# Two-layer hybrid decoder trunk: causal masks of four blocks moved to TensorE, linear unit's copies reordered, some low parts moved between VectorE and GpSimd

## Chip, cores and metric

One core of a Trainium2 chip. The time of an execution is device microseconds of the slowest core, here the only one. A kernel's time is the median of its runs. Some single executions were also recorded by the hardware profiler, and every row below comes from such a record.

## What is computed

Two residual layers over 1024 tokens of width 1024, all in float32 on the outside. In each layer the input is RMS-normalised, projected, mixed, gated, projected back and added.

```python
# layer 0: sliding-window attention and a state-space layer, side by side
ssm = s5_mixer(...) * silu(gate_b)       # s5_mixer ends with a gated linear unit:
#   h = gelu(y) @ glu_w + glu_b ;  h[..., :W] * sigmoid(h[..., W:])
h = h + concat([att * silu(gate_a), ssm]) @ w_out
# layer 1: an indexer scores all causal keys, the best 256 of each query are attended
score = sum_h w_h * relu(qi_h . ki)              # 8 index heads
_, idx = top_k(where(key <= query, score, -1e30), 256)
logits = where(valid, q . k * Dh**-0.5 + bias[query - key], -1e30)
h = h + (softmax(logits) @ v * silu(gate)) @ w_out
```

Layer 1 has 8 query heads of width 128 on 2 key heads. The kernel doesn't gather the selected keys. It computes the logits of all causal keys and adds a mask that makes those of unselected or later keys hugely negative.

## The kernel before

**Arithmetic.** Every float32 operand of a large matmul is split in two: `hi` is the operand rounded to the matmul's type (fp32r) and `lo = x - hi`. A product is three matmuls into one PSUM tile: hi.hi, hi.lo, lo.hi. So each operand costs a copy to `hi`, on ScalarE, and a subtraction for `lo`, on VectorE or GpSimd.

**Weights.** All weights come through one stream of 39 chunks of 1024 x 256 (class `Stream`, `load_w` at L134). The load goes to `wraw`; then `piece` writes `whi` on ScalarE (L153) and `wlo` (L154) on the engine that the tuple `LO_ON_V` (L126) names by the chunk's number: VectorE if the number stands there, GpSimd else. A chunk takes four pieces of 2 of its 8 rows of tiles (512 columns each). Chunks 0 to 8 are the input projection of layer 0, 9 and 10 the linear unit, 11 to 18 the output projection of layer 0, 19 to 30 the input projection of layer 1 and 31 to 38 its output projection. Within layer 1 the order is: two chunks for the indexer, then `PROJ1 = "a01kv23bcd"`, of which a to d are gate chunks and 0 to 3 query chunks. So chunk 22 is query chunk "0" and 23 is "1"; 24 and 25 are keys and values, 29 and 30 the gate chunks "c" and "d". The `hi` and `lo` of a chunk are made while the chunk before it is multiplied.

**Order.** TensorE's order is the program's own in the later stages (`manual_schedule`). The order of the other engines' instructions is laid out by a list scheduler which simulates a time line; `high_priority`, `behind(insts)` (L128, an instruction isn't queued ahead of those named) and `issue_after` bend it. Each engine then runs its queue strictly in order. All DMAs are issued by SyncE.

**The linear unit (L856 to L889).** Two chunks, each times two halves of the tokens, each times two tiles: eight groups of 24 matmuls of 512 columns (L872 to L874), two PSUM tiles a step. For each step ScalarE takes a tanh of one tile (L879), VectorE multiplies (L880, L881, the latter reading the second tile), ScalarE writes the high part (L882) and VectorE the low part (L883) of `cat[half]`, rows 4 to 7. In the list here a "GLU group" is one pass of `i` and `half`, two steps; they are counted 0 to 3, and groups 1 and 3 are the second half of the tokens. After the loop the attention branch's rows 0 to 3 of `cat` are loaded from DRAM (tile `at`, 4 buffers), copied on ScalarE (L888) and subtracted on VectorE (L889), eight times. Their pool is then closed, and the projection that follows (L895 to L925) loads the residual's tiles `xh` from DRAM into the space; VectorE adds a PSUM tile to one at L911. Its matmuls are L218 to L220 and L232 to L234, the helpers of all projections, in groups of 24.

**The indexer and the search.** TensorE makes the index scores (L1064, L1065), ScalarE the relu (L1067), VectorE the weighted sum (L1072), for blocks of 128 queries 2 to 7 (blocks 0 and 1 have at most 256 causal keys, so all are selected). Then a binary search of 32 steps finds each query's 256th score: blocks 3, 5, 7 on VectorE (class `OnV`, L1204; its count at L1221 writes a tile `vjunk` that nobody reads), blocks 2, 4, 6 on ScalarE and GpSimd (`OnS`, L1244; L1257, L1261). Bits of the scores are flipped ahead of it through a tile `flip` (L1198 to L1200). `tie_mask` (L1282) then writes `mk[b]`, bfloat16, 0 for a selected key and about 1e25 for another. All this runs beside the input projection of layer 1, whose head norms are made by ScalarE and GpSimd (`norm_heads`, L384: ScalarE squares at L389, GpSimd L199 and L200, ScalarE L392), and whose results are transposed on TensorE (L1151) and copied on ScalarE (L1153).

**Attention of layer 1.** A unit is a block of 128 queries with one of the two key heads, four query heads. `dsa_scores` (L1350): the bias of a head is loaded by a strided DMA into `bt`; GpSimd puts the mask into it, for blocks 0 and 1 by adding `mk0` to the diagonal's 128 columns (L1372), for others by subtracting `mk[b]` (L1374); TensorE makes the logits (three matmuls, L1375 to L1377, in one of 3 PSUM tiles `pq`); VectorE adds the bias, negates and takes the running minimum in one instruction (L1379); ScalarE takes the exponential (L1385); VectorE takes the reciprocal and, for two of four heads, normalises (L1390; ScalarE does the other two). Then TensorE transposes the probabilities (L1401), ScalarE and VectorE split them (L1404, L1405), and TensorE multiplies with the values (L1415 to L1417). The order of units: blocks 0 to 3 with key head 0, blocks 0 to 3 with key head 1, then blocks 4 to 7 with both. The scores of the first two units are made ahead (`first_units`, L1491, tiles of a pool `gat`), beside the projection of gate chunk "d". The scores of a later unit are made two units ahead of its values. `q1T_hi` and `q1T_lo` are the queries' parts (L1336 on ScalarE, L1337 on GpSimd for all but the first two units).

**Outputs.** The gated results of the first eight units are kept in tiles (`gat1`). At unit 8 `first_half` (L1595) closes the pool of the first half and calls `to_aT` (L1522) for all eight: ScalarE writes `aT_hi` (L1524), VectorE `aT_lo` (L1525), 512 columns each. The output projection of the first half (`out_pieces`, L1550 to L1552, 256 columns a matmul) then fills TensorE between the matmuls of blocks 4 to 7. Those of the second half call `to_aT` from `finish`.

## Time and profile before

| what | value |
| --- | --- |
| runs | 1068.32, 1062.63, 1068.51 us; median 1068.32 us |
| profiled execution | 1065.89 us, of which the recorded span is 1064.2 us |
| granted TensorE clock, mean of the span | 0.987 of full speed |
| busy share of TensorE / weight loads / VectorE / ScalarE / GpSimd | 95% / 84% / 70% / 58% / 41% |
| instructions | 19143 |
| DMA | 138.33 MB, mean 130 GB/s |

All times are microseconds from the start of the span unless marked ns. PE is the TensorE matmul, PEld its weight load (which overlaps), DVE VectorE, ACT ScalarE, POOL GpSimd, SP SyncE. A line L154 is line 154 of the kernel. In an instruction's row, `out<-in` are the program's tile names with partitions x elements; in square brackets stands the time for which the engine had been idle before it and the instruction that ended the idle time. `xN` counts instructions. Matmuls are pipelined, so that one's duration can be longer than the distance to the next, and some rows join several neighbours.

### The profile page before, as it was taken

How to read it: one execution, taken by the hardware profiler on the slowest of the kernel's cores; microseconds unless marked ns; L12 is line 12 of the kernel's file. 1: busy time of each engine (PE TensorE's matmuls, PEld its weight loads, DVE VectorE, ACT ScalarE, POOL GpSimd, SP SyncE). 2: the span in 40 equal slices, each digit the busy share in tenths (PEclk: the TensorE clock that was granted, in tenths of full speed). 3: DMA queues.
4: the chain of work that ended last, by engine and by line, in shares of the span. 5: the costliest groups of instructions: out<-in, count | busy, mean ns of one | idle time of the engine just before them, and what ended most of it. 6: DMA issues, size and time to landing. Idle time of an engine off the chain costs nothing.

```text
span 1064.2 us, 19143 instructions
## 1 busy us (share of the span) xinstructions
PE 1013.1 (95%) x6536; PEld 890.5 (84%) x6536; DVE 748.7 (70%) x1705; ACT 622.3 (58%) x1671; POOL 436.5 (41%) x722
## 2 busy tenths in 40 slices
PE   7899999999998999999999989999998889999998
PEld 5798999999864588877789989999886669898898
DVE  6628889973796554544667578888877986777742
ACT  7543653222787433434566989789967865565620
POOL 5897632221000002122041678678545847456000
PEclk9999999999999999999999999999999989999999
DMA  7282455339462317531020232122436644665333
GB/s 267 95 284 80 105 163 163 107 105 276 133 198 60 100 60 267 207 119 61 1 89 21 75 98 68 41 68 86 121 112 212 204 123 142 201 190 162 117 100 119
DMA packets 103697, 138.33 MB, mean 130 GB/s; under 512 B 9352, under 2 KB 79880, under 8 KB 98736
## 3 DMA queue, kind: packets, MB, share of 16 engines
q1 hardware_dynamic: 103600, 137.12, 41.3%
q8 instruction: 51, 0.84, 0.3%
q14 instruction: 46, 0.38, 0.1%
HBM read 102.31 MB, written 36.21 MB: 130 GB/s over the span
## 4 chain that ended last, share of the span: by engine, by line
PE 68%; DVE 14%; POOL 6%; ACT 5%; DMA 3%; issue 3%; SPq 1%; ACTq 0%; POOLq 0%; DVEq 0%
PE mm L234 8%; PE mm L232 8%; PE mm L233 8%; PE mm L218 5%; PE mm L219 5%; PE mm L220 5%; PE mm L1551 3%; PE mm L1552 3%; PE mm L1550 3%; PE psx L801 2%; PE tr L1401 2%; PE mm L1416 1%; PE mm L1417 1%; PE pq L1375 1%; PE tr L795 1%
## 5 line engine op out<-in xcount | busy, mean ns | idle before, releaser
L153 ACT CAST whi<-wraw 128x512 fp32r<-128x512 f32 (+1 forms) x152 | 87.3, 643 | 74.4 <-PE mm L233 38.2
L154 POOL TENSOR_TENSOR wlo<-wraw,whi 128x512 fp32r<-128x512 f32 x64 | 87.3, 1391 | 96.3 <-ACT whi L153 96.3
L219 PE MATMUL mm<-wlo,h1T_hi 128*128 128x256 f32 x384 | 110.3, 288 | 0.0
L218 PE MATMUL mm<-whi,h1T_hi 128*128 128x256 f32 x384 | 109.8, 288 | 0.2 <-DVE gst L981 0.2
L220 PE MATMUL mm<-whi,h1T_lo 128*128 128x256 f32 x384 | 109.6, 287 | 0.0
L1374 POOL TENSOR_TENSOR bt<-bt,mk 128x384 f32<-128x384 f32 (+3 forms) x80 | 82.5, 1049 | 61.9 <-DMA bt<-g_d 43.9
L919 POOL TENSOR_TENSOR acc<-acc,sq 128x512 f32<-128x512 f32 x12 | 18.1, 1507 | 195.4 <-DVE wlo L154 154.0
L1221 DVE TENSOR_SCALAR_CACHE_REDUCE vjunk<-sc,vt 128x512 bf16<-128x512 uint16 (+5 forms) x90 | 91.0, 1012 | 2.7
L232 PE MATMUL mm<-hT_hi,whi 128*128 128x256 f32 (+1 forms) x288 | 85.6, 297 | 0.0
L234 PE MATMUL mm<-hT_hi,wlo 128*128 128x256 f32 (+1 forms) x288 | 85.6, 297 | 0.0
L233 PE MATMUL mm<-hT_lo,whi 128*128 128x256 f32 (+1 forms) x288 | 85.5, 297 | 0.0
L1257 ACT ACTIVATE sjunk<-sc,st 128x384 bf16<-128x384 uint16 (+5 forms) x90 | 77.7, 864 | 6.2 <-POOL st L1261 4.2
L1550 PE MATMUL mm<-aT_hi,whi 128*128 128x256 f32 x256 | 73.5, 287 | 1.2 <-ACT aT_hi L1524 1.2
L218 PEld LDWEIGHTS mm<-whi,h1T_hi 128*128 128x128 f32 x384 | 72.9, 191 | 1.0 <-PE psi L1065 0.6
L219 PEld LDWEIGHTS mm<-wlo,h1T_hi 128*128 128x128 f32 x384 | 73.2, 191 | 0.4
L154 DVE TENSOR_TENSOR wlo<-wraw,whi 128x512 fp32r<-128x512 f32 (+1 forms) x88 | 62.9, 760 | 15.1 <-ACT whi L153 12.7
L1551 PE MATMUL mm<-aT_lo,whi 128*128 128x256 f32 x256 | 72.7, 284 | 0.7 <-DVE aT_lo L1525 0.7
L220 PEld LDWEIGHTS mm<-whi,h1T_lo 128*128 128x128 f32 x384 | 72.9, 190 | 0.4
L1552 PE MATMUL mm<-aT_hi,wlo 128*128 128x256 f32 x256 | 72.6, 284 | 0.0
L1385 ACT ACTIVATE s<-s,mn 128x384 f32<-128x384 f32 (+7 forms) x56 | 46.0, 821 | 30.9 <-DVE mn L1379 30.9
L1072 DVE SCALAR_TENSOR_TENSOR sc<-relu,wi,sc 128x384 f32<-128x384 f32 (+3 forms) x70 | 49.6, 711 | 20.3 <-ACT relu L1067 16.6
L392 ACT ACTIVATE st<-mm,nr 128x64 f32<-128x64 f32 (+1 forms) x160 | 46.0, 360 | 30.1 <-POOL nr L200 29.9
(398 smaller groups left out, 3478.7 us busy)
## 6 DMA issues: line engine op xcount, KB each, us to landing
wraw<-in_w_dram SPq DMA_DIRECT2D x20, 1024.0 KB, 5.0
wraw<-in_wo_dram SPq DMA_DIRECT2D x16, 1024.0 KB, 5.2
bt<-g_d SPq DMA_DIRECT2D x24, 256.0 KB, 4.6
g_d<-g1r_d SPq DMA_DIRECT2D x8, 576.0 KB, 10.8
bt<-g_d SPq DMA_DIRECT2D x24, 192.0 KB, 3.4
qT_d<-gst SPq DMA_DIRECT2D x32, 128.0 KB, 1.9
qT<-qT_d SPq DMA_DIRECT2D x32, 128.0 KB, 3.9
xh<-in_xT_dram SPq DMA_DIRECT2D x16, 256.0 KB, 5.7
```

What stands on the lines that cost most here:

```text
L153: S.copy(hi[p_], raw[p_])
L154: eng.tensor_sub(lo[p_], raw[p_], rd(hi[p_]))
L218: T.matmul(ps, a, hi[:, k, c0:c1], start=(k == 0), stop=False)
L219: T.matmul(ps, a, lo[:, k, c0:c1], start=False, stop=False)
L220: T.matmul(ps, b, hi[:, k, c0:c1], start=False, stop=(k == 7))
L232: T.matmul(o, a, hT[0][:, k, ts], start=(k == 0), stop=False)
L233: T.matmul(o, a, hT[1][:, k, ts], start=False, stop=False)
L234: T.matmul(o, b, hT[0][:, k, ts], start=False, stop=(k == 7))
L1221: V.tensor_scalar(junk[:, :128 * (b + 1)], data(b), self.thr(j), None, op0=OP.is_ge, op1=OP.add, accum_out=self.cnt[:, it, j:j + 1])
L1550: T.matmul(ps, a, aT[0][:, k, toks], start=(k == 0), stop=False)
L1551: T.matmul(ps, a, aT[1][:, k, toks], start=False, stop=False)
L1552: T.matmul(ps, b, aT[0][:, k, toks], start=False, stop=(k == 7))
```

## The change

Five edits:

1. `LO_ON_V` gets 22 and 23: the low parts of query chunks "0" and "1" are made on VectorE instead of GpSimd.
2. In the linear unit the instruction of the high and of the low part that each GLU group issued last is remembered. The copies and subtractions of the attention branch are queued behind those of group 1 (first half of the tokens) or group 3 (second half).
3. The unread output of the count on VectorE shares the tile `flip` instead of having `vjunk`.
4. The masks of blocks 0 and 1 become one bfloat16 tile of 128 x 256, 0 in its left half and 1e25 above the diagonal in its right one. For blocks 0 to 3 GpSimd no longer touches `bt`; the group of logit matmuls begins with one more, of the negated identity in bfloat16 with `mk[b]`, which puts the negated mask into PSUM. Blocks 4 to 7 stay as they were.
5. `to_aT` takes an engine for the low part; in `first_half` the first four of the eight units get GpSimd.

```diff
--- before.py
+++ after.py
@@ -123,7 +123,7 @@
 
     wcount = [0]
     raw_pools = [wp]
-    LO_ON_V = (0, 1, 2) + tuple(range(9, 21)) + (29, 30) + tuple(range(33, 39))
+    LO_ON_V = (0, 1, 2) + tuple(range(9, 21)) + (22, 23) + (29, 30) + tuple(range(33, 39))
 
     def behind(insts):
 
@@ -853,6 +853,7 @@
         ca = tuple(cps[1 - half].tile([128, 8, 512], F32R, name=f"cat_{n}") for n in ("hi", "lo"))
         cat.append(ca)
     gbt = yp.tile([128, 4, L], F32, name="gbt")
+    glu_last = []
     for n in range(4):
         dma(gbt[:, n], gb_d[n])
     for i in range(2):
@@ -879,14 +880,18 @@
                 S.activation(sg, pp[0], AF.Tanh, scale=0.5, bias=glub[:, 1, 4 + n:5 + n])
                 V.scalar_tensor_tensor(sg, sg, 1.0, gt_, op0=OP.add, op1=OP.mult)
                 V.scalar_tensor_tensor(sg, pp[1], glub[:, 0, n:n + 1], sg, op0=OP.add, op1=OP.mult)
-                S.activation(ca[0][:, 4 + n], sg, AF.Copy, scale=0.25)
-                V.scalar_tensor_tensor(ca[1][:, 4 + n], sg, 0.25, rd(ca[0][:, 4 + n]), op0=OP.mult, op1=OP.subtract)
+                glu_hi = S.activation(ca[0][:, 4 + n], sg, AF.Copy, scale=0.25)
+                glu_lo = V.scalar_tensor_tensor(ca[1][:, 4 + n], sg, 0.25, rd(ca[0][:, 4 + n]), op0=OP.mult,
+                                                op1=OP.subtract)
+            glu_last.append((glu_hi.ins, glu_lo.ins))
     for half in range(2):
         for g in range(4):
             at = st3.tile([128, 512], F32, name="at", bufs=4)
             dma(at, att_d[g, :, half * 512:(half + 1) * 512])
-            S.copy(cat[half][0][:, g], at)
-            V.tensor_sub(cat[half][1][:, g], at, rd(cat[half][0][:, g]))
+
+            with behind(glu_last[1 + 2 * half]):
+                S.copy(cat[half][0][:, g], at)
+                V.tensor_sub(cat[half][1][:, g], at, rd(cat[half][0][:, g]))
     es_y.close()
     es_3.close()
     es_h1 = ExitStack()
@@ -1217,7 +1222,7 @@
             if it % 16 == 0:
                 self.t = self.start()
             for j, b in enumerate(self.blocks):
-                junk = tk.tile([128, L], BF16, name="vjunk")
+                junk = tk.tile([128, L], I32, name="flip").bitcast(BF16)
                 V.tensor_scalar(junk[:, :128 * (b + 1)], data(b), self.thr(j), None, op0=OP.is_ge, op1=OP.add,
                                 accum_out=self.cnt[:, it, j:j + 1])
             i = it % 16
@@ -1317,11 +1322,15 @@
     if "sc7" in dbg:
         dma(dbg["sc7"], sc[7])
 
-    mk0 = mp.tile([128, 128], F32, name="mk0")
+
+    mk01 = mp.tile([128, 256], BF16, name="mk01")
     with tc.issue_after(ki_lo.ins):
-        G.memset(mk0, 0.0)
-    G.affine_select(out=mk0, in_=mk0, pattern=[[-1, 128]], compare_op=OP.is_ge, fill=NEG,
+        G.memset(mk01, 0.0)
+    G.affine_select(out=mk01[:, 128:], in_=mk01[:, 128:], pattern=[[-1, 128]], compare_op=OP.is_ge, fill=FAR,
                     base=0, channel_multiplier=1)
+    mk[0], mk[1] = mk01[:, 128:], mk01
+    nid = mp.tile([128, 128], BF16, name="nid")
+    V.tensor_scalar(nid, ident, -1.0, None, op0=OP.mult)
 
     def dsa_q_load(b, kv):
         qr = akv.tile([128, 4, 128], F32, name="q1r", bufs=2)
@@ -1367,12 +1376,12 @@
                     bp_ = fp if b < 4 and nbt[0] > 6 and nbt[0] % 2 else pool_
                     bt = bp_.tile([128, 512], F32, name="bt", bufs=6)[:, :n]
                 last_ttr[1] = dma(bt, skewed(h, 1023 - 128 * b + c0, n)).ins
-                with behind(last_rstd):
-                    if b < 2:
-                        G.tensor_add(bt[:, w - 128:], bt[:, w - 128:], mk0)
-                    else:
+                if b < 4:
+                    T.matmul(o, nid, mk[b][:, ks], start=True, stop=False)
+                else:
+                    with behind(last_rstd):
                         G.tensor_sub(bt, bt, mk[b][:, ks])
-                T.matmul(o, qT[0][:, g], kT[0][:, kv, ks], start=True, stop=False)
+                T.matmul(o, qT[0][:, g], kT[0][:, kv, ks], start=b > 3, stop=False)
                 T.matmul(o, qT[0][:, g], kT[1][:, kv, ks], start=False, stop=False)
                 T.matmul(o, qT[1][:, g], kT[0][:, kv, ks], start=False, stop=True)
 
@@ -1519,10 +1528,10 @@
     def gated(o, gv):
         V.scalar_tensor_tensor(gv, o, 0.5, gv, op0=OP.mult, op1=OP.mult)
 
-    def to_aT(b, kv, gv, aT):
+    def to_aT(b, kv, gv, aT, eng=V):
         qc = slice((b % 4) * 128, (b % 4 + 1) * 128)
         S.copy(aT[0][:, 4 * kv:4 * kv + 4, qc], gv)
-        V.tensor_sub(aT[1][:, 4 * kv:4 * kv + 4, qc], gv, rd(aT[0][:, 4 * kv:4 * kv + 4, qc]))
+        eng.tensor_sub(aT[1][:, 4 * kv:4 * kv + 4, qc], gv, rd(aT[0][:, 4 * kv:4 * kv + 4, qc]))
 
     def out_pieces(half, aT, ahead=None):
 
@@ -1597,8 +1606,8 @@
         ap_.append(es_a.enter_context(tc.tile_pool(name="att_l", bufs=1, reuse_waits="tile")))
         aT = attn_T()
         with tc.issue_after(last_ttr[0]):
-            for u in first:
-                to_aT(*u, aT)
+            for i, u in enumerate(first):
+                to_aT(*u, aT, G if i < 4 else V)
         fill.gen, fill.owed = out_pieces(0, aT), 0.0
 
     wstream.lazy = True
```

## Rows read from the trace of the kernel before

**Rows 1.** The page's first part: busy us, share of the span, instructions.

```profile
PE 1013.1 (95%) x6536; PEld 890.5 (84%) x6536; DVE 748.7 (70%) x1705; ACT 622.3 (58%) x1671; POOL 436.5 (41%) x722
```

**Rows 2.** The page's fourth part: the chain that ended last, by engine.

```profile
PE 68%; DVE 14%; POOL 6%; ACT 5%; DMA 3%; issue 3%; SPq 1%; ACTq 0%; POOLq 0%; DVEq 0%
```

**Rows 3.** By stage: length, busy per engine, granted clock, DMA share, GB/s.

```profile
621.00:630.00 9.00, 6.07 (x38) 5.74 (x37) 8.54 (x22) 5.05 (x18) 7.17 (x19) 0.81 0.46 147
626.00:790.00 164.00, 164.00 (x1167) 154.25 (x1166) 136.73 (x300) 144.19 (x428) 115.00 (x269) 0.99 0.25 79
811.20:866.50 55.30, 46.62 (x237) 36.74 (x238) 46.47 (x135) 41.45 (x102) 43.11 (x47) 0.94 0.66 208
866.50:878.00 11.50, 8.22 (x40) 7.32 (x39) 9.55 (x24) 7.91 (x16) 3.34 (x4) 0.70 0.38 103
```

**Rows 4.** Timelines of 353 to 412: start, duration, instruction, [idle before].

```profile
358.08 0.62 ACT L888 CAST cat_hi<-at 128x512 fp32r<-128x512 f32 x1 [5.26 <-DMA at<-att_d]
...
364.14 0.50 PE L872 MATMUL mm<-y_hi,whi 128*128 128x512 f32 x1 [2.19 <-DVE sg L881]
...
367.54 0.50 PE L872 MATMUL mm<-y_hi,whi 128*128 128x512 f32 x1 [0.34 <-ACT sg L879]
...
402.75 0.69 DVE L911 TENSOR_TENSOR xh<-mm,xh 128x512 f32<-128x512 f32 x1 [6.05 <-DMA xh<-in_xT_dram]
```

**Rows 5.** Steps of the chain that ended last: start, duration, line.

```profile
315.50 1.86 PE psx L801 x4
...
392.90 0.24 PE mm L232
```

**Rows 6.** GpSimd's timeline of 495 to 660, and TensorE's wait of 540 to 740.

```profile
545.47 5.77 POOL L154 TENSOR_TENSOR wlo<-wraw,whi 128x512 fp32r<-128x512 f32 x4 [5.40 <-ACT whi L153]
...
582.48 5.43 POOL L154 TENSOR_TENSOR wlo<-wraw,whi 128x512 fp32r<-128x512 f32 x4 [14.04 <-ACT whi L153]
...
PE tr L1151 <- ACT st L392: 2.9, 1, 2.9
```

**Rows 7.** VectorE: the group of L154 (busy us, mean ns) and its timeline near 550.

```profile
L154 DVE TENSOR_TENSOR wlo<-wraw,whi 128x512 fp32r<-128x512 f32 x84 | 58.0, 738 | 12.8 <-ACT whi L153 12.7
...
548.70 2.89 DVE L1072 SCALAR_TENSOR_TENSOR sc<-relu,wi,sc 128x320 f32<-128x320 f32 x2
552.24 1.20 DVE L1072 SCALAR_TENSOR_TENSOR sc<-relu,wi,sc 128x320 f32<-128x320 f32 x2
```

**Rows 8.** Groups and a wait of 811 to 866; the last row's group 785 to 811.

```profile
L1374 POOL TENSOR_TENSOR bt<-bt,mk 128x320 f32<-128x320 f32 (+2 forms) x30 | 28.2, 964 | 9.7 <-DMA bt<-g_d 9.2 <-DVE s L1390 0.3
...
L1337 POOL TENSOR_TENSOR q1T_lo<-q1r,q1T_hi 128x512 fp32r<-128x512 f32 x9 | 11.9, 1324 | 11.8 <-ACT q1T_hi L1336 11.8
...
L1372 POOL TENSOR_TENSOR bt<-bt,mk 128x128 f32<-128x128 f32 x8 | 3.6, 480 | 0.0
...
L1390 DVE TENSOR_SCALAR s<-s,den 128x384 f32<-128x384 f32 x4 | 4.1, 1047 | 0.0
...
L1390 DVE TENSOR_SCALAR s<-s,den 128x256 f32<-128x256 f32 x2 | 1.7, 849 | 0.1
...
DVE s L1379 <- POOL bt L1374: 1.3, 2, 0.7
...
L1390 DVE TENSOR_SCALAR gat<-gat,den 128x256 f32<-128x256 f32 x2 | 0.6, 352 | 0.0
```

**Rows 9.** TensorE's timeline of 809 to 813.

```profile
811.24 0.44 PE L1375 MATMUL pq<-k1T_hi,q1T_hi 128*128 128x384 f32 x1 [1.33 <-ACT q1T_hi L1336]
```

**Rows 10.** Timelines of 850 to 878: TensorE, VectorE and GpSimd.

```profile
869.80 0.41 PE L1375 MATMUL pq<-k1T_hi,q1T_hi 128*128 128x320 f32 x1 [1.39 <-DVE mn L1379]
872.62 0.79 PE L1416 MATMUL mm<-pT_lo,v_hi 128*128 128x512 f32 x1 [1.89 <-DVE pT_lo L1405]
...
868.06 1.28 DVE L1525 TENSOR_TENSOR aT_lo<-gat,aT_hi 128x512 fp32r<-128x512 f32 x2
...
872.10 0.79 POOL L1374 TENSOR_TENSOR bt<-bt,mk 128x320 f32<-128x320 f32 x1 [5.71 <-DVE aT_lo L1525]
```

## Prediction

> **What bounds the kernel now.** I read the page's busy shares first: TensorE has work in 95% of the span [rows 1], so only time in which TensorE waits, or runs at its lower clock, can be won, and every matmul that is added has to find such time. The chain that ended last says where that time is: 68% of it is TensorE, 14% VectorE, 6% GpSimd [rows 2]. The table by stage then shows that the lost time is not spread evenly. From 626 to 790 us TensorE is busy in all 164.00 us: nothing done there on other engines can shorten it, and what is won ahead of it is carried through. Three of the places that the change touches lose: 621 to 630 (TensorE busy 6.07 of 9 us, mean granted clock 0.81), the attention of the first four blocks (811.2 to 866.5, 46.62 of 55.3, clock 0.94) and the stretch in which the first half's outputs are split (866.5 to 878, 8.22 of 11.5, clock 0.70) [rows 3]. The fourth, the linear unit, I read wait by wait in the timelines of its engines [rows 4]; the prices of single instructions come from the groups by line and the waits of a stage.
>
> **A, the linear unit's order.** ScalarE stands in program order in front of the first att copy (L888) for 5.26 us until its load has landed; behind it queue L882 and L879, on VectorE L883 and L881, and those free the PSUM tiles. So TensorE waits 2.19 us for L881 at 364.14 and 0.34 us for L879 at 367.54 [rows 4]. With the att copies queued behind GLU groups 1 and 3 both waits go: 2.5 us. What is late instead: the last four copies and four subtractions now follow the last GLU step, some 4 x 0.6 = 2.4 us, and the load of `xh` may wait that long for their tiles. Its first use on VectorE already waits 6.05 us, until 402.75 [rows 4], but TensorE needs a PSUM tile back only three groups of 24 matmuls after 392.90, the start of the projection on the chain: 3 x 24 x 0.24 (the 512-column matmul there [rows 5]) = 17.3 us, at 410.2. That leaves 7 us for the 2.4. **A = -2.5 us**; with the cover gone it would be 0.
>
> **B, chunks 22 and 23 on VectorE.** Counting the four-piece bursts of L154 on GpSimd from chunk 21 on, 22 is the burst at 545.47, 23 the one at 582.48 and 24 the next. They hold GpSimd for 5.77 and 5.43 us [rows 6], and the head norms (L199, L200) queue behind it. From 582 to 625 the chain runs beside TensorE: burst 23, then norms, then ScalarE, then burst 24, then norms, until TensorE gets a transpose after a wait of 2.9 us [rows 6]; the granted clock then falls, mean 0.81 over 9 us, which is 9 x 0.19 = 1.7 us of lost columns [rows 3]. Without burst 23 ScalarE and GpSimd are up to 5 us earlier at burst 24, more than the 2.9 us by which they were late. VectorE pays 8 pieces x 0.74 = 5.9 us [rows 7]. But its own instructions are slowed while GpSimd runs a burst: two of 320 columns take 2.89 us at 548.70 against 1.20 us at 552.24, behind the burst [rows 7], so about 1.7 us a burst, 3.4 us in two, comes back. The net 2.5 us falls before 613, where VectorE waits for ScalarE's relu anyway. Bounds: -4.6 (all of 2.9 + 1.7) to +1 (VectorE holds the relu tiles up near 545). I take -4.0, near the full sum, since the late norms have one visible cause. **B = -4.0 us.** Sharing the tile `flip` adds no wait of an engine on another: counts and flips are both VectorE's. At worst the first counts of two blocks move behind the last flip (under 2 us), which TensorE, fully busy there, doesn't see.
>
> **C, the masks on TensorE.** Removed: 32 additions on GpSimd. In the stage 811 to 866 that is 8 of L1372 and 16 of the 30 of L1374 [rows 8], together 8 x 0.48 + 16 x 0.96 = 19 us of an engine that was busy 43.11 of 55.3 [rows 3]. GpSimd itself is rarely waited for (DVE for bt 1.3 us, [rows 8]); the gain is on VectorE, busy 46.47 of 55.3. Its normalisation L1390 takes 849 ns for 256 columns in this stage against 352 ns for the same shape ahead of it, and 1047 ns for 384 [rows 8]. The two of 256 lose 0.5 us each; the four of 384, with 0.45 us (an estimate, a little above the 352) as their own price, 0.6 each; with what the smallest lose I put 4 us. With the 1.3 us wait that is 5.3 us of VectorE, and VectorE holds much of the chain here.
>
> The Trainium skill (SBUF — State Buffer, "SBUF: two separate sides") says that VectorE and GpSimd take a shared port pair by an exclusive lock, held for a whole instruction. The trace agrees for L1390 (849 against 352 ns). By that rule the subtractions that the change puts on GpSimd lock VectorE out in their turn, which is rival 2: the time would be its 1059.4 us instead of the 1054.7 that I take.
>
> Added: 32 matmuls, 4 x 2 x (128 + 256 + 384 + 512) = 10,240 columns, bf16 on bf16, a kind that no row shows. Cheap end: 0.24 us for 512 columns; dear end: 1.86 / 4 = 0.465 us, as the slowest 512-column matmul [rows 5]: 4.8 to 9.3 us. I take the cheap end, as the masks enter beside matmuls that keep that pitch at the full clock. Of it 1536 columns, 0.7 us, fall to the first two units (795 to 804), where TensorE then waits 1.33 us at 811.24 for ScalarE anyway [rows 9], so about 0.3 us counts; the other 4.1 us fall into the stage, where TensorE has 55.3 - 46.6 = 8.7 us idle. About a third of the chain there is TensorE's, so 1.4 to 2 us of it count. **C = -5.3 + 1.8 + 0.3 = -3.2 us**, bounds -9 to +6.
>
> **D, four low parts on GpSimd.** VectorE's eight L1525 stand between TensorE and what it waits for: 1.39 us for L1379 at 869.80 and 1.89 us for L1405 at 872.62; four of them (two took 1.28 us at 868.06 [rows 10]) are 2.5 us. After the waits the clock is low (mean 0.70 to 878), 11.5 x 0.3 = 3.5 us. Full gain: 2.5 + about 2 of clock. Against it: GpSimd takes 1.32 us for this subtraction [rows 8], 5.3 us for four. It is idle for 5.71 us up to 872.10 [rows 10], so its queue bears them, but VectorE's remaining four would run beside them, and L1390's 849 against 352 ns tells what that can cost. I take **D = -2.0 us**, bounds -5 to +2.
>
> **Sum.** -2.5 - 4.0 - 3.2 - 2.0 = -11.7 us against the profiled execution's 1065.9 us (span 1064.2 and 1.7 around it): 1054.2. The median of the three runs is 2.4 us above that execution and the lowest 3.3 below; I add half a microsecond and say 1054.7 us, of which the range holds the doubt.
>
> **Rivals.** 1. The masks set TensorE's pace (slower side). Each group's first matmul now stands on the path from a freed PSUM tile to VectorE. A matmul that starts behind a wait took 0.50 us [rows 4]; the stage gets 24, 12.0 us, VectorE then waits for TensorE, and its 5.3 us are worth nothing. With D void too and the first two units at 1.4 us: -2.5 - 4.0 + 12.0 + 1.4 = +6.9, 1073.3 us. It decides from the point where a mask matmul costs over 0.29 us on the path (7 us / 24). For it: TensorE is at 95%. Against: 8.7 us idle in the stage.
>
> 2. The port: GpSimd's 5.3 us in D lock out VectorE's four L1525 and the L1390 beside them, and q1T_lo and the other bt go on doing so in the stage: C gives 0 and D 0. Then A + B = -6.5, 1059.4 us. For it: 849 against 352 ns. Against: the masks, most of GpSimd's work there, go.
>
> 3. The relief is worth more: VectorE's chain in the stage shortens by its whole 5.3 us and TensorE's lower clock (0.94 x 55.3: 3.3 us) mostly goes, D gives 4.5: -2.5 - 4.6 - 8 - 4.5 = -19.6, 1046.3 us.
>
> 4. A does nothing, because the late `xh` loads make TensorE wait what it saved: -9.2, 1056.7 us.
>
> **How the numbers follow.** Forecast 0.50 (own range 1049 to 1060), rival 1 0.12, rival 2 0.18, rival 3 0.12, rival 4 0.08. The range 1045 to 1068 leaves out the upper part of rival 1 and a little below rival 3. One per cent is about what a measurement of this kernel can tell from no change; against the median of 1068.3 it lies at 1057.6. Faster by more: 0.38 of the forecast, all of rival 3, half of rival 4: 0.54. Slower by over 1% (1079) needs rival 1 and a bad new order besides: 0.06. The rest, 0.40, is within 1%.
>
> **What would show it.** A: no wait at L872, the last L889 near 395. B: the 2.9 us wait at L1151 gone, clock 1.0 from 600 to 790, bursts of L154 on VectorE. C: L1390 near 350 ns for 256 columns, the stage 811 to 866 some 3 us shorter, mask matmuls at 0.23 us for 512 columns. D: no wait of TensorE above 1 us where the outputs are split, and a clock above 0.85 there. The forecast is wrong if the stage of the first blocks gets longer, or if a new wait of TensorE stands between 626 and 790.

## The result, and the profile after

The changed kernel takes 1058.26 us (median of 7 runs, 1055.13 to 1060.39) against 1067.86 us for the kernel before in the same comparison (7 runs, 1062.63 to 1069.52): ratio 0.992, 95% interval 0.9899 to 0.9941. That is 9.6 us less by the medians, 8.5 by the ratio. The forecast was 1054.7 us in a range of 1045 to 1068; of the three chances it falls to "within 1%", by a little.

The page of the changed kernel, its first and fourth part:

```profile
PE 1009.5 (96%) x6568; PEld 888.7 (84%) x6568; DVE 748.0 (71%) x1710; ACT 621.6 (59%) x1671; POOL 403.7 (38%) x686
...
PE 70%; DVE 13%; POOL 5%; DMA 4%; ACT 4%; issue 3%; SPq 1%; ACTq 0%; POOLq 0%; DVEq 0%
```

TensorE has 32 matmuls more, GpSimd 36 instructions and 32.8 us less [rows 1]. The stages that answer to [rows 3], moved by TensorE's lead (columns as there):

```profile
616.00:625.00 9.00, 6.75 (x43) 6.42 (x42) 8.58 (x21) 6.48 (x24) 7.24 (x21) 0.81 0.45 147
621.00:785.00 164.00, 164.00 (x1165) 154.23 (x1165) 140.11 (x304) 142.83 (x425) 110.97 (x264) 0.99 0.24 78
806.70:859.30 52.60, 47.65 (x263) 37.32 (x264) 43.98 (x135) 41.84 (x103) 23.48 (x24) 0.97 0.68 215
859.30:870.80 11.50, 7.51 (x41) 6.64 (x40) 9.15 (x20) 7.62 (x15) 9.71 (x9) 0.85 0.36 101
```

The first row is a surprise: the stretch that part B was to mend still has a granted clock of 0.81. The third is shorter by 3.0 us (811.2 to 866.8 took 55.6 before). The last has a better clock, yet TensorE is busy for less of it.

Where the time went is best read from four instructions that every kernel here has, by their starts in the timelines. I take the first matmul of the projection behind the linear unit (L232, 392.7 before), the first logit matmul of all (L1375, 795.1), the ninth, with which the stage of the first blocks begins (811.2), and the one that is the 41st, the first of block 4 with its second key head (866.8). Each is given as its distance from the one ahead of it, the first from the linear unit's restart at 353.3, the last column up to the start of the last matmul:

| kernel | linear unit | to first logits | first units | first blocks | behind them |
| --- | --- | --- | --- | --- | --- |
| before | 39.4 | 402.4 | 16.1 | 55.6 | 193.9 |
| changed | 36.4 | 399.7 | 16.9 | 52.6 | 193.4 |
| linear unit alone | 36.5 | 403.4 | 16.0 | 54.9 | 192.7 |
| chunks alone | 39.2 | 401.3 | 20.2 | 55.0 | 192.5 |
| masks alone | 40.5 | 402.4 | 17.8 | 53.4 | 192.8 |
| split alone | 40.3 | 400.8 | 16.1 | 54.5 | 195.1 |
| changed, low parts all on VectorE | 36.5 | 399.7 | 16.9 | 53.3 | 192.8 |
| changed, low parts all on GpSimd | 36.5 | 399.6 | 16.9 | 53.1 | 196.8 |
| linear unit + chunks | 36.5 | 401.5 | 17.3 | 55.0 | 194.3 |
| changed + chunk 24 | 36.5 | 395.2 | 25.5 | 54.6 | 193.4 |
| the same, search one step shorter | 36.5 | 395.4 | 16.6 | 53.2 | 195.8 |

Each row is one profiled execution. Up to the linear unit the executions differ by -1.1 to +2.9 us though nothing there was changed, which is why the stages are compared and not the spans, and a stage still scatters by a microsecond or two, as its clock falls once more or less. So, from the unrounded starts, the changed kernel won 3.1 us in the linear unit, 2.7 up to the first logits and 3.0 in the first blocks, lost 0.7 in the first units, and won 0.5, which is nothing, behind them.

### The profile page after: what moved, and what is told of

It reads as the page before. It is cut to its first block, busy times and chain, and to the rows that moved or that the text cites. A ratio compares the mean times of both kernels' runs of the same rounds, so it can differ in the third digit from the quotient of the medians.

```text
span 1056.1 us, 19160 instructions
## 1 busy us (share of the span) xinstructions
PE 1009.5 (96%) x6568; PEld 888.7 (84%) x6568; DVE 748.0 (71%) x1710; ACT 621.6 (59%) x1671; POOL 403.7 (38%) x686
## 4 chain that ended last, share of the span: by engine, by line
PE 70%; DVE 13%; POOL 5%; DMA 4%; ACT 4%; issue 3%; SPq 1%; ACTq 0%; POOLq 0%; DVEq 0%
PE mm L234 8%; PE mm L232 7%; PE mm L233 7%; PE mm L218 4%; PE mm L219 4%; PE mm L220 4%; PE mm L1560 3%; PE mm L1561 3%; PE mm L1559 3%; PE tr L1410 2%; PE psx L801 2%; PE mm L1425 1%; PE mm L1426 1%; PE pq L1384 1%; PE pq L1386 1%
## 5 line engine op out<-in xcount | busy, mean ns | idle before, releaser
L154 POOL TENSOR_TENSOR wlo<-wraw,whi 128x512 fp32r<-128x512 f32 x56 | 76.5, 1394 | 76.7 <-ACT whi L153 76.7
L1226 DVE TENSOR_SCALAR_CACHE_REDUCE flip<-sc,vt 128x512 bf16<-128x512 uint16 (+5 forms) x90 | 91.0, 1012 | 2.6
L1383 POOL TENSOR_TENSOR bt<-bt,mk 128x320 f32<-128x320 f32 (+3 forms) x64 | 66.8, 1060 | 58.0 <-DMA bt<-g_d 36.3
L232 PE MATMUL mm<-hT_hi,whi 128*128 128x256 f32 (+1 forms) x288 | 85.6, 297 | 0.0
L154 DVE TENSOR_TENSOR wlo<-wraw,whi 128x512 fp32r<-128x512 f32 (+1 forms) x96 | 66.1, 732 | 14.3 <-ACT whi L153 13.9
L392 ACT ACTIVATE st<-mm,nr 128x64 f32<-128x64 f32 (+1 forms) x160 | 45.7, 357 | 27.8 <-POOL nr L200 27.6
L1413 ACT CAST pT_hi<-tr 128x512 fp32r<-128x512 f32 x72 | 41.5, 578 | 33.9 <-PE tr L1410 31.9
```

Of the source, the lines that this page charges most:

```text
L154: eng.tensor_sub(lo[p_], raw[p_], rd(hi[p_]))
L232: T.matmul(o, a, hT[0][:, k, ts], start=(k == 0), stop=False)
L1226: V.tensor_scalar(junk[:, :128 * (b + 1)], data(b), self.thr(j), None, op0=OP.is_ge, op1=OP.add, accum_out=self.cnt[:, it, j:j + 1])
```

## The experiments

**1. The linear unit's order alone.** L880 to L889 as in the change, nothing else.

```diff
-                S.activation(ca[0][:, 4 + n], sg, AF.Copy, scale=0.25)
+                glu_hi = S.activation(ca[0][:, 4 + n], sg, AF.Copy, scale=0.25)
...
+            with behind(glu_last[1 + 2 * half]):
```

> The kernel before with the linear unit's new order alone. My theory: the two waits at L872 (2.19 and 0.34 us) go and nothing takes their place, so the run is 2.5 us under the kernel before, and TensorE is ahead by 2.5 us when the output projection of layer 0 begins and keeps this to the end. Rival (the late loads of xh take it back): no wait at L872, but TensorE's lead is gone at 420 us and the time is that of the kernel before. Second rival (the gain is given back at the wait for L392 near 625, which GpSimd's bursts set): the lead of 2.5 us holds to 610 and falls under 1 us by 640.

Measured: 1062.32 us against 1066.33, ratio 0.9963 (0.9943 to 0.9982). The two waits at L872 [rows 4] are gone: TensorE's waits from 340 to 400 us are down to one line (what waited, for whom; total, times, longest):

```profile
PE tr L795 <- DVE pT L798: 1.5, 2, 0.9
```

The stage is 2.9 us shorter. Counted from the linear unit's restart, TensorE is still 2.0 us ahead at the ninth logit matmul (3.1 by the spans' own times, of which 1.1 were there before the stage began). My theory holds in the main and the first rival falls. The second names a place where about 1 us is given back: the wait for L392 is 2.9 us as before, but the mean granted clock behind it, from 620.1 to 626.9, is 0.50, where before it was 0.75 from 625.4 to 632.2. That is one execution, and the lead did not fall under 1 us.

**2. The chunks alone.**

```diff
-    LO_ON_V = (0, 1, 2) + tuple(range(9, 21)) + (29, 30) + tuple(range(33, 39))
+    LO_ON_V = (0, 1, 2) + tuple(range(9, 21)) + (22, 23) + (29, 30) + tuple(range(33, 39))
```

> The kernel before with the low parts of chunks 22 and 23 on VectorE and nothing else. In the changed kernel the wait at L1151 stayed (2.3 us) and so did the stretch at the lower clock behind it; ahead of it stands the burst of chunk 24 on GpSimd, and the search has been put beside it. My theory: the burst of chunk 24 owns that wait, so this edit brings 1 to 2.5 us, and the wait at L1151 is still over 2 us. Rival (as predicted): the wait was owned by the burst of chunk 23; without the other edits' shift the wait and the lower clock go, and the run is 4 us faster.

Measured: 1068.71 against 1066.33 us, ratio 1.0011 (0.9994 to 1.0029): no gain. TensorE's waits at L1151 were 4.5 us in all, so the rival falls. But 1.1 us were won up to the first logits, and 4.1 lost again in the first units. There TensorE waits 2.05 us for VectorE, and from 798.7 to 805.5 the mean granted clock is 0.50 (1.00 over the same 6.8 us before), which is 6.8 x 0.5 = 3.4 us of columns. That place was in neither theory.

**3. The masks alone** (with the shared `flip`).

```diff
+                if b < 4:
+                    T.matmul(o, nid, mk[b][:, ks], start=True, stop=False)
...
-                junk = tk.tile([128, L], BF16, name="vjunk")
+                junk = tk.tile([128, L], I32, name="flip").bitcast(BF16)
```

> The kernel before with the masks of blocks 0 to 3 on TensorE and the shared tile flip (the masks' tiles need its space). My theory: the first two units cost 1 us more, the stage of the first blocks gets 3 us shorter because VectorE's normalisation no longer runs beside GpSimd's mask work; together 2 to 3 us under the kernel before, and the normalisation of 256 columns near 0.58 us. Rival (the port's relief needs the other edits, the masks alone only load TensorE): the stage is not shorter and the run is 0 to 2 us above the kernel before.

Measured: 1066.18 against 1066.33 us, ratio 1.0 (0.9977 to 1.0023). Neither theory is clean: the first blocks got 2.2 us shorter, as in mine, but the first units took 1.7 us longer.

**4. The split alone.**

```diff
-                to_aT(*u, aT)
+                to_aT(*u, aT, G if i < 4 else V)
```

> The kernel before with four of the eight low parts of the first half's outputs on GpSimd and nothing else. My theory: VectorE's other four take 1.3 us each instead of 0.64 while GpSimd works, so VectorE is done no sooner and the wait for L1405 grows as much as the wait for L1379 shrinks: 0 us, within half a microsecond either way. Rival (the prediction's): VectorE's queue is 2 us shorter and TensorE's waits between 866 and 878 fall from 3.3 to about 1 us: 2 us faster.

Measured: 1066.32 against 1066.33 us, ratio 0.9996 (0.9977 to 1.0014). The two waits of [rows 10], 3.3 us, became one of 3.6 us for L1405, as in my theory.

**5 and 6. The changed kernel with all eight low parts on VectorE, and all eight on GpSimd** (`V`, or `G`, in place of `G if i < 4 else V`).

> The changed kernel with all eight low parts of the first half's outputs back on VectorE. My theory (the split gains nothing, because each of VectorE's low parts beside GpSimd's takes twice its time): the time of the changed kernel within 1 us, TensorE's waits between 857 and 870 again some 3.3 us in two pieces. Rival (the split is worth 2 us): 2 us above the changed kernel.

> The changed kernel with all eight low parts on GpSimd. My theory: GpSimd needs 8 x 1.47 = 11.8 us, VectorE's few instructions beside it each wait for one of GpSimd's, and the mask subtractions of block 4 and the first output matmul queue behind: TensorE waits 4 us or more longer than in the changed kernel, 3 to 7 us slower. Rival (VectorE's queue was the only thing in the way): VectorE is free 4.6 us sooner, the wait for L1414 (3.6 us in the changed kernel) goes, and the run is 2 to 3 us faster.

Measured against the same runs of the kernel before (1065.58 us): all on VectorE 1059.21, ratio 0.9946 (0.9924 to 0.9968); all on GpSimd 1060.31, ratio 0.9949 (0.9926 to 0.9971). Both lie 2.8 to 3.1 us above the changed kernel's 0.992 by the ratios, with overlapping intervals, so these times alone don't exclude that the split is worth 2 us. The traces speak against it: with all eight on VectorE the waits are back as 1.37 and 1.89 us, where the split has one of 3.62, and the stretch behind the first blocks is no longer (192.8 against 193.4 us).

With all eight on GpSimd the wait of 3.62 us is gone, as in the rival, but a longer one comes 15 us later. VectorE, GpSimd and TensorE:

```profile
871.57 8.18 DVE L1399 TENSOR_SCALAR s<-s,den 128x640 f32<-128x640 f32 x1
...
881.40 0.55 DVE L1399 TENSOR_SCALAR s<-s,den 128x640 f32<-128x640 f32 x1
...
877.61 1.79 POOL L1383 TENSOR_TENSOR bt<-bt,mk 128x384 f32<-128x384 f32 x2
...
880.87 0.79 PE L1425 MATMUL mm<-pT_lo,v_hi 128*128 128x512 f32 x1 [5.78 <-DVE pT_lo L1414]
```

One normalisation on VectorE takes 8.18 us, the next of the same shape 0.55. It ends at 879.75; GpSimd worked from 861.03 to 879.40 without a gap that the profile shows, its queue of low parts, masks and weights being longer now. In no other trace here does an instruction of this kind take over 1.8 us. The stretch behind the first blocks is about 3.5 us longer than in the changed kernel, as I expected (3 to 7), but this execution (1063.53 us) is 3.2 us above the median of its 12 runs, and against all eight on VectorE the ratios differ by 0.3 us only. How often the long wait comes, these runs don't show.

**7. Chunk 24 on VectorE too.**

```diff
-    LO_ON_V = (0, 1, 2) + tuple(range(9, 21)) + (22, 23) + (29, 30) + tuple(range(33, 39))
+    LO_ON_V = (0, 1, 2) + tuple(range(9, 21)) + (22, 23, 24) + (29, 30) + tuple(range(33, 39))
```

> The changed kernel with the low parts of chunk 24 on VectorE too. My theory: the burst of L154 at 611 on GpSimd owns the wait of 2.3 us at L1156; without it the head norms come in time, the wait and the lower clock behind it (1.7 us) go: 3 to 4 us under the changed kernel. Rival (VectorE becomes the one that is late, as it is busy 9.5 of 10 us there): the wait stays over 1.5 us, now behind VectorE's L154, or moves to the next chunk; within 1 us of the changed kernel.

Measured: 1065.57 against 1065.58 us, ratio 1.0008 (0.999 to 1.0027). The whole gain of the changed kernel is gone, although the wait at L1156 and the low clock behind it went, as my theory said: TensorE led by 9.4 us at the first logits and by 0.1 at the ninth.

**8. Without the mask matmuls** (the masks of blocks 0 to 3 are left out of the computation).

```diff
-                if b < 4:
-                    T.matmul(o, nid, mk[b][:, ks], start=True, stop=False)
...
```

> The changed kernel without the mask matmuls: the masks of blocks 0 to 3 are left out of the computation. It prices the 32 matmuls. My theory: their 10,240 columns at 0.23 us for 512 are 4.7 us of TensorE's time, of which about half lies in waits: 2 to 3 us under the changed kernel, near 1 us of it in the first two units. Rival (they set TensorE's pace): 5 us or more under it. Other rival (hidden in waits for VectorE): within 1 us.

Measured: 1057.76 us, ratio 0.9927 (0.9901 to 0.9953), the changed kernel's 0.992. The 32 matmuls are hidden: the first units take 16.3 us without them and 16.9 with them, the first blocks 52.8 and 52.6. The rival that they are hidden holds.

**9. Linear unit and chunks, without masks and split** (the edits of 1 and 2 together).

> The kernel before with the linear unit's new order and chunks 22 and 23 on VectorE, without the masks and the split. Alone, the order brought 4.0 us and the chunks lost 1.2 us. In the run of the chunks alone TensorE had won 1 us by 789 and lost 4.9 between 789 and 803, where VectorE, in the middle of the chain of the selection masks, stood 4.1 us for a TensorE group. First theory (that loss comes from where the scheduler puts the last gate's and the first units' instructions among the mask chain, and the masks on TensorE change this): the loss returns, and the run is about 3 us under the kernel before. Second theory (the loss came from TensorE being late against the mask chain by chance of that order, and the linear unit's order mends it): TensorE leads by 5 us at 789 and keeps it at 812; 5 to 7 us under the kernel before, and the masks and the split add 2 to 3 us more to make the changed kernel.

Measured: 1065.94 against 1067.44 us, ratio 0.9985 (0.9967 to 1.0003). The first theory is the nearer one: the 5 to 7 us of the second lie outside the interval. But of the loss in the first units 1.2 us returned, not 4.1; TensorE's wait for VectorE is there again (2.05 us), the low clock of experiment 2 is not (mean 1.00 from 794 to 812). By the two ratios the chunks take back more than half of what the linear unit brought, though the intervals of experiments 1 and 9 overlap. Masks and split together, worth nothing alone, make the step from 0.9985 to 0.992; the changed kernel without the split stands at 0.9946 (experiment 5), so by the ratios more than half of the step is the masks' edit.

**10. The selection masks in another order.**

```diff
-    for b in range(2, NT):
+    for b in ON_V + ON_S:
         tie_mask(b, *found[b])
```

> The changed kernel with the selection masks made in the order 3, 5, 7, 2, 4, 6 instead of 2 to 7. VectorE's searches end 5.7 us before ScalarE's (763.2 against 768.9), so the chain of masks can start sooner. My theory: that chain (L1297 to L1307) sets when the second unit's queries can be split (q1T_hi, 0.6 us behind the last mask in every run so far) and with it the stage of the first blocks. Its end comes 3 to 5 us sooner, but TensorE's own work ends 1.35 us before that, so only 1 to 2 us are won: 1 to 2 us under the changed kernel. Rival (TensorE's own work sets it): the wait for q1T_hi is gone or the same, and the time is within half a microsecond of the changed kernel. Second rival (ScalarE's search is delayed by the mask instructions put among it): the last mask is no sooner, 0 to 2 us slower.

Measured: 1063.1 us, ratio 0.9966 (0.9945 to 0.9986): slower than the changed kernel. The last mask came no sooner (805.3 against 805.7), although the search was not delayed (it ended at 769.0 instead of 768.9), and TensorE stood 3.84 us for VectorE in the first unit. The second rival named the effect, but neither its cause nor its size.

**11. Experiments 7 and 10 together.**

> The changed kernel with chunk 24 on VectorE too and the masks in the order 3, 5, 7, 2, 4, 6. With chunk 24 alone TensorE led the kernel before by 9.5 us at 789 and by nothing at 812: it waited 2.7 us for VectorE and 5.1 us for q1T_hi, behind the mask chain. My theory (the chain is the wall): with the chain earlier the lead is kept in part, and the run is 4 us or more under the run with chunk 24 alone, about the time of the changed kernel or 1 to 3 us under it. Rival (chunk 24 loads VectorE and ScalarE, and these are slower whatever the order): the lead is lost again between 789 and 812 and the run is within 1.5 us of the one with chunk 24 alone.

Measured: 1062.83 us, ratio 0.9956 (0.994 to 0.9972), against 1.0008 with chunk 24 alone. The lead at the ninth logit matmul was 2.8 us instead of 0.1, as the last mask came at 807.9 instead of 810.6. So the lead is kept in part, as in my theory, but the run stays above the changed kernel, where I had expected its time or less. TensorE still waits 5.82 us for `q1T_hi` there.

**12. Chunk 24, and the search one step shorter.**

```diff
-    for it in range(16, 32):
+    for it in range(16, 31):
...
```

> The changed kernel with chunk 24 on VectorE too and the binary search one step shorter (31 of 32 steps; the last bit of each query's threshold is left out of the computation). A step takes 251 us / 32 = 7.8 us on ScalarE's side. My theory (search and mask chain are the wall that takes chunk 24's gain): the last mask comes 6 to 8 us sooner, the wait for q1T_hi (5.1 us) goes, TensorE keeps 6 us or more of its lead of 9.5 us at 812; 5 us or more under the run with chunk 24 alone and 1 to 4 us under the changed kernel. Rival (TensorE loses it through VectorE's order around the first units): the waits for VectorE stay, and the run stays within 2 us of the one with chunk 24 alone.

Measured: 1057.02 us, ratio 0.9903 (0.9876 to 0.993). What changed is the wait for the end of the search: the last mask is done at 802.8 instead of 810.6, the wait for `q1T_hi` fell from 5.1 to 1.0 us, that of 2.7 us for VectorE in the first unit went too, and TensorE kept 7.5 of its 7.9 us of lead. This is my theory. Against the changed kernel the two intervals overlap, so nothing is won that could be claimed.

## Why the prediction was right or wrong

**The premise that failed: a second chain.** The prediction read "TensorE is busy in all 164.00 us" as "what is won ahead of it is carried through". It is carried only as far as the search comes along. The search ends on ScalarE, then six selection masks follow one another through the one tile `flip`, and the queries of the third attention unit, the first behind `first_units`, are split only behind the last of them. ScalarE's timeline, of the kernel before and of the changed one:

```profile
809.53 1.15 ACT L1302 ACTIVATE mk<-flip,top 128x1024 bf16<-128x1024 f32 x1 [0.41 <-DVE den L1386]
810.59 0.60 ACT L1336 CAST q1T_hi<-q1r 128x512 fp32r<-128x512 f32 x1
```

```profile
804.56 1.15 ACT L1307 ACTIVATE mk<-flip,top 128x1024 bf16<-128x1024 f32 x1 [0.73 <-DVE den L1395]
806.01 0.60 ACT L1345 CAST q1T_hi<-q1r 128x512 fp32r<-128x512 f32 x1
```

In both, TensorE's ninth logit matmul waits 1.3 us for this copy ([rows 9], and 806.67 after). TensorE and the mask chain arrive within some 1.3 us of each other; a gain counts only if both get it. The linear unit's order moves both, as the search starts from scores that TensorE makes later (in experiment 1 the search ends at 770.6, before at 773.6). Chunk 24 moved TensorE alone. Of its lead of 9.4 us, 4.0 end in this wait, 2.9 in one for VectorE in the first unit, whose reductions stand behind a mask's instructions, and the rest between the two, with the granted clock at 0.50 from 791.3 to 794.7. With a shorter search the lead comes back (experiments 7 and 12):

```profile
789.74 0.22 PE L1380 MATMUL pq<-mk,nid 128*128 128x128 bf16 x1 [2.69 <-DVE mn L1388]
...
790.62 0.38 SPq L1337 DMA_DIRECT2D q1r<-q_d  x1
...
808.19 0.60 ACT L985 ACTIVATE mm<-gst 128x512 f32<-128x512 f32 x1 [2.94 <-DVE gst L984]
...
809.44 1.15 ACT L1307 ACTIVATE mk<-flip,top 128x1024 bf16<-128x1024 f32 x1 [0.65 <-DVE flip L1302]
810.50 0.60 ACT L1345 CAST q1T_hi<-q1r 128x512 fp32r<-128x512 f32 x1
...
811.15 0.69 PE L1384 MATMUL pq<-k1T_hi,q1T_hi 128*128 128x384 f32 x1 [5.10 <-ACT q1T_hi L1345]
```

```profile
801.65 1.15 ACT L1307 ACTIVATE mk<-flip,top 128x1024 bf16<-128x1024 f32 x1 [0.73 <-DVE den L1395]
803.11 0.60 ACT L1345 CAST q1T_hi<-q1r 128x512 fp32r<-128x512 f32 x1
...
803.76 0.44 PE L1384 MATMUL pq<-k1T_hi,q1T_hi 128*128 128x384 f32 x1 [1.04 <-ACT q1T_hi L1345]
```

In the last three rows of each, the same instructions a step apart: the mask, the copy a microsecond behind it, the matmul behind that. Only the mask's time and the length of TensorE's wait differ.

The copy reads nothing of the mask. In experiment 7 its load `q1r`, issued at 790.62, landed 3.1 us later, and ScalarE stood idle for 2.94 us up to 808.19, yet the copy began at 810.50: its place in ScalarE's queue is behind the last mask. No run put it ahead. So the runs show that the wait follows the search and its masks, and not how much of it is need and how much is the queue's order.

**A, the linear unit (-2.5): right.** 3.1 us in the changed kernel's stage, 2.9 alone; the run alone is 3.9 us faster by its ratio (interval 1.9 to 6.1). The cover held as computed: VectorE's last subtraction of the attention rows ends at 396.5 in the changed kernel, and its first `xh` addition still waits 3.64 us for its load. What the sum left out, about half a microsecond, is not settled; in two kernels whose linear unit was as before the clock fell once in that stage, in the one profiled before not, so some executions may lose more there.

**B, the chunks (-4.0): wrong, the step that names the wait's owner.** The prediction gave the wait of 2.9 us at L1151 to burst 23. It is burst 24's. The changed kernel, first GpSimd's timeline, then TensorE's wait from 535 to 735:

```profile
611.48 5.04 POOL L154 TENSOR_TENSOR wlo<-wraw,whi 128x512 fp32r<-128x512 f32 x4
...
618.48 0.71 POOL L200 TENSOR_TENSOR nr<-nr,neghalf 128x2 f32<-128x2 f32 x1
```

```profile
PE tr L1156 <- ACT st L392: 2.3, 1, 2.3
```

Bursts 22 and 23 are gone, 24 still stands in front of the head norms, and the wait is 2.3 us instead of 2.9. The prediction had reckoned that burst 24 would come up to 5 us earlier and that this would do. It did come 5.4 us earlier (616.84 in the trace before), but TensorE, 4 to 5 us ahead itself, needed the norms that much earlier too. Taking burst 24 away removed the wait and the low clock altogether: from 621 to 785 the mean granted clock is then 1.00 (experiment 7).

So the 2.7 us that the stage won lie for the most part elsewhere. Between the same matmuls in the traces before and after, TensorE's lead grows by 1.2 us near 550, where two waits for the indexer's relu (0.59 and 0.21 us before, right behind burst 22) are gone and one of 0.31 has come, by 0.9 up to 603, and by only 0.5 where the prediction had reckoned nearly all of it, 2.9 + 1.7 us. That the size came out near is luck.

Alone, the chunks brought nothing at all. The loss stands in the first units, in the middle of the mask chain, but not in the wait for the copy, which is shorter here (0.55 us in experiments 2 and 9). Two things went wrong, both from the order in which the scheduler laid out the queues. In experiment 9, VectorE and TensorE:

```profile
787.40 0.69 DVE L985 SCALAR_TENSOR_TENSOR gst<-mm,gst 128x512 f32<-128x512 f32 x1 [3.23 <-ACT mm L984]
...
795.14 2.02 DVE L1299 TENSOR_TENSOR_SCAN flip<-ones_b,sg 128x896 f32<-128x896 bf16 x1
797.08 0.27 DVE L1383 CUSTOM_DVE_ANT_0 gat<-pq,st 128x128 f32<-128x128 f32 x1
...
797.41 0.33 PE L1379 MATMUL pq<-k1T_hi,gat 128*128 128x128 f32 x1 [2.05 <-DVE mn L1383]
```

VectorE stands 3.23 us for a gate's tanh on ScalarE with the next scan of the mask chain queued behind it; and the first unit's reductions (L1383 here) are queued behind a scan of 2.02 us, so that TensorE waits 2.05 us for a PSUM tile. In the changed kernel the same scan stands behind three of these reductions:

```profile
790.58 0.28 DVE L1388 CUSTOM_DVE_ANT_0 gat<-pq,st 128x128 f32<-128x128 f32 x1
...
791.77 2.02 DVE L1300 TENSOR_TENSOR_SCAN flip<-ones_b,sg 128x896 f32<-128x896 bf16 x1 [0.26 <-ACT sg L1299]
```

Experiment 2 shows the same two marks as 9 (3.24 us at 789.28, a scan ahead of the first reduction) and the low clock behind them, and experiment 10 a wait of 3.84 us of the same kind. So the chunks' 2.7 us were seen only together with the masks' edit. Which part of that edit brings the better order, the matmuls, GpSimd's work that goes, or the shared `flip`, was not separated, and the linear unit's order with the masks but without the chunks was not run: what the chunks add to these two stays open. The prediction had taken the shared tile for nearly free ("under 2 us"). VectorE's first counts move by much more, from 531.5 to 610.1, but its search still ends no later (763.2, before 766.1), and TensorE, as predicted, doesn't see it there.

**C, the masks (-3.2): the mechanism right, two sizes off, and worth nothing alone.** The changed kernel's groups by line in the first blocks, and, in the second fence, TensorE's timeline at two logit groups:

```profile
L1380 PE MATMUL pq<-mk,nid 128*128 128x512 bf16 x8 | 3.1, 388 | 0.0
...
L1399 DVE TENSOR_SCALAR s<-s,den 128x384 f32<-128x384 f32 x4 | 2.5, 637 | 0.0
...
L1399 DVE TENSOR_SCALAR s<-s,den 128x256 f32<-128x256 f32 x2 | 1.2, 576 | 0.0
```

```profile
813.58 0.38 PE L1380 MATMUL pq<-mk,nid 128*128 128x512 bf16 x1
...
814.50 0.39 PE L1380 MATMUL pq<-mk,nid 128*128 128x512 bf16 x1
```

The columns were priced rightly: from one group's mask to the next it is 0.92 us for four matmuls of 512 columns, 0.23 each. What counts of them on the path, 1.8 us in the sum, is about nothing (experiment 8, by its stages). VectorE's relief was overrated: the normalisation of 256 columns fell from 849 to 576 ns, of 384 from 1047 to 637 [rows 8], that is 2 x 0.27 + 4 x 0.41 = 2.2 us where the sum had 3.4 for these six. The stage's 3.0 us hold besides this the wait for `bt` (1.3 us before, none after) and one fall of the clock less, near 850; they are not to be told apart further. The clock alone doesn't make it: experiment 9, without the masks' edit, took 55.0 us at a mean granted clock of 1.00. Rival 1, the masks setting TensorE's pace, is out.

**D, the split (-2.0): wrong.** Rival 2's mechanism is what happens, at this place. The changed kernel, VectorE, GpSimd and TensorE:

```profile
860.57 1.32 DVE L1534 TENSOR_TENSOR aT_lo<-gat,aT_hi 128x512 fp32r<-128x512 f32 x1
861.81 0.54 DVE L1388 CUSTOM_DVE_ANT_0 s<-pq,bt,mn 128x320 f32<-128x320 f32 x1
...
862.28 1.29 DVE L1534 TENSOR_TENSOR aT_lo<-gat,aT_hi 128x512 fp32r<-128x512 f32 x1
...
863.90 1.34 DVE L1534 TENSOR_TENSOR aT_lo<-gat,aT_hi 128x512 fp32r<-128x512 f32 x1
865.16 1.28 DVE L1414 TENSOR_TENSOR pT_lo<-tr,pT_hi 128x512 fp32r<-128x512 f32 x2
...
858.79 5.90 POOL L1534 TENSOR_TENSOR aT_lo<-gat,aT_hi 128x512 fp32r<-128x512 f32 x4
...
865.90 0.50 PE L1425 MATMUL mm<-pT_lo,v_hi 128*128 128x512 f32 x1 [3.62 <-DVE pT_lo L1414]
```

VectorE's low parts take 1.32, 1.29 and 1.34 us as long as GpSimd makes its own, and 0.68 before ([rows 10]: two in 1.28). Four of them and half a queue cost what eight had cost, `pT_lo` comes no sooner, and TensorE's 1.39 + 1.89 us became 3.62. Counted from the 41st logit matmul, the matmul that waits for `pT_lo` starts after 6.6 us in the changed kernel and in experiment 4, and after 5.8 before and in experiment 5, with all eight on VectorE. The clock, 0.70 before, is 0.85 over that stretch, as it fell for a shorter time. That isn't the split's: over 19 us from 0.8 us ahead of the 41st logit matmul the mean is 0.91 in the changed kernel and in experiment 5, which has no split, and 0.82 before and in experiment 4, which has it.

**The sum.** By the stages of the two traces A brought 3.1, B 2.7, C 3.0 - 0.7 = 2.2 (from unrounded starts) and what lies behind 0.5, together 8.5 us where the prediction had 11.7. Of the difference of 3.2 us B makes 1.3, D 1.5 and C 1.0, and A gives 0.6 back. That B and C bring this only together was in no case of the prediction, and of the signs that it named, B's (the wait gone, a clock of 1.0 from 600 to 790) and D's (no wait above 1 us) did not show. A small slip in it changes nothing: the forecast and rival 1 are counted from 1065.9 + 0.5 us, rivals 2 to 4 from 1065.9.

## What to carry to other kernels

An engine that is busy in every microsecond of a stretch is not yet the only bound of it: ask what else must be finished at the stretch's end, or stands ahead of it in another engine's queue, follow that chain back, and count a gain only as far as both arrive earlier. Where a scheduler lays out the queues from a simulated time line, an edit also moves instructions that it doesn't touch; single edits then need not add up (by the ratios -3.9, +1.2, 0.0 and -0.4 us alone, -8.5 together here), and a part is judged in the company in which it will run. Handing half of a row of two-input subtractions from VectorE to GpSimd gained nothing here, as both ran side by side.

## What the runs showed of the hardware

VectorE's subtraction with both operands in SBUF takes 1.3 us beside GpSimd's of the same kind against 0.68 alone, while its instructions with one operand in PSUM keep their time beside GpSimd: L1388 takes 0.48 us at 863.50, as at 869.26 in the trace before with GpSimd idle, and L1414 1.28 us for two. The Trainium skill (SBUF — State Buffer, "SBUF: two separate sides") has the distinction: its lock concerns a VectorE instruction with two SBUF inputs, or one in a 2-port mode. The trace agrees on the two inputs, and it adds that GpSimd pays as well: its four took 5.90 us there, 1.48 each, and 1.30 each in experiment 6, where VectorE had none of these. The normalisation L1399 reads one tile in SBUF and is slowed too (576 ns for 256 columns in the first blocks, 352 [rows 8]); whether it runs in such a mode no trace says. It can also be held for longer than one instruction of GpSimd: 8.18 us in experiment 6, against 0.55, while GpSimd went from one to the next without a gap that the profile shows. A bfloat16 matmul at the head of a group of fp32r ones keeps their pitch, 0.23 us for 512 columns.
